# Pair results and two quarters of the token-major shares turned by DMA in a decoder trunk

## The chip, the cores and the metric

One core of one Trainium2 chip runs the whole kernel. The core has a TensorE (PE in the profile; PEld are its weight loads), a VectorE (DVE), a ScalarE (ACT), a GpSimd (POOL) and a SyncE (SP), which here only issues transfers; 16 DMA engines move data. The metric is the device time of the kernel in microseconds. Before the change it is 1678.69 us, the median of three runs (1678.51 to 1679.63).

## The reference

Two layers of a decoder trunk over 512 tokens of width 1024, in fp32:

```python
x = x + 0.5 * swiglu(rms_norm(x), wg1, wu1, wd1)       # feed-forward width 2816
z = rms_norm(x) @ w_in                                  # q, k, v and three conv parts
x = x + concat([attention(q, k, v), conv(...)]) @ w_out # sliding window 128, sinks, ALiBi
x = x + 0.5 * swiglu(rms_norm(x), wg2, wu2, wd2)
```

with `swiglu(h) = (silu(h @ wg) * (h @ wu)) @ wd` and a last RMSNorm after the two layers. So there are four feed-forwards. Nearly all the work is in their three weight matrices.

## The kernel before, in words

**Products.** Activations are held with features on the partitions ("feature-major", 128 features by 512 tokens a chunk); `xpair` holds the running x so, in four tiles of two chunks. Each fp32 factor is split in two: a rounded high part and the rest. A product is three matmuls (high x high, high x low, low x high). For the weights `split` (L212) does this: ScalarE casts the raw weight to `wh` (L213), VectorE subtracts to `wl` (L214). Three buffers each of `wh` and `wl` let the splits run two products ahead.

**Seven products for eight.** Most of a feed-forward is done by a scheme of Strassen's kind (as Winograd wrote it): 2 x 2 blocks of weights and activations are multiplied with seven block products, listed in `CHAINS` (L65). A stage therefore has seven *steps*, and each step two halves with 12 matmuls each per 128 columns of the other operand. `class Seven` (L554) makes the activation forms a step needs (`b11`, `b21`, `t1` to `t4`, `b22`), each split again by ScalarE and VectorE; `need_split` makes the weight forms, partly by transfers that add (issued by POOL, L208 and L279) and partly by VectorE (L249, L281).

**Stages of a feed-forward.** The lists `FIRST`, `INNER` and `LAST` (L32 to L40) name them. `p` and `d` are plain products up and down. A `w` stage (`winograd2`, L992), here called a *pair*, multiplies two blocks of the gate and up matrices; its results `ups[0..3]` come out *token-major* (128 tokens by 512 features each). An `s` stage (`share`, L822), a *shared stage*, multiplies two such pairs' results by the down matrix. The first feed-forward (`FIRST`) has four pairs, then one of another form (`u`) whose result needs no turning, and two shared stages. The two of `INNER` have five pairs and two shared stages; pairs 1, 3, 5 and 7 feed these, and pair 9 goes into the last plain down product. The last (`LAST`) has four such pairs as well, and its pair 9 goes into the closing stage `e`.

**Turning.** The down product needs its activations feature-major, so `turn` (L1047) turns each pair's result on TensorE: 16 transposes of 128 x 128 (L1050) into PSUM, then for pairs that feed shared stages a copy by ScalarE (L1057) into `raws[b]`, a tile of the pool `g8` (four buffers). For pair 9 of an inner feed-forward the PSUM tile is split straight into high and low (L1062). The 16 transposes are queued in `pending` and spread by `flush` over steps 0, 1 and 2 of the next pair (or over the next plain down product, or the next shared stage).

**Shares by tokens.** In the inner feed-forwards the shared stages' products come out token-major as well: `class Apart` (L856) sums them over both stages in eight tiles `y[t, o]`. Its `back(o, t)` (L870) turns one quarter (one half of the features, one half of the tokens) with eight transposes (L877) and adds it to x on VectorE (L883). `BACK_AT` puts three quarters into steps 2, 5 and 6 of the second shared stage, and the fourth follows in the last down product.

**What sets the order.** Each engine works through its own queue in order. A compile-time scheduler fills these queues: it takes the instructions in program order as priority, simulates when their inputs and buffers are ready, and moves an instruction ahead where its engine would be free. `tc.issue_after(i)` pins what is traced under it behind instruction `i` on that instruction's engine. SP issues all plain weight loads (L196) in its queue order, each as soon as one of the eight `raw` buffers is free. The pools that matter here are `g2` (14 tiles of 128 x 512 words), `g8` (4 tiles four times as large) and `xf` (14 tiles of 4 KB a partition).

Of the kernel before, what the change touches and what calls it, by code (L numbers as in the profile page):

```python
# [8 lines left out]
F32 = mybir.dt.float32  # L9
F32R = mybir.dt.float32r  # L10
BF16 = mybir.dt.bfloat16
I32 = mybir.dt.int32
AF = mybir.ActivationFunctionType
ALU = mybir.AluOpType

P = 128
D = 1024
S = 512
# [34 lines left out]

BACK_AT = {2: (0, 0), 5: (1, 1), 6: (1, 0)}
SCORES_AT = (5, 6, 7, 8, 9, 10, 12, 13)
# [16 lines left out]
def trunk_kernel(  # L72
# [55 lines left out]
    def f32(ap):  # L128
        return ap.bitcast(F32)


# [80 lines left out]
    def split(hi, lo, raw, eng=nc.vector):  # L212
        nc.scalar.copy(hi, raw)  # L213
        eng.tensor_sub(lo, raw, f32(hi))  # L214

    def split_far(hi, lo, raw):
# [5 lines left out]
    def need_split(g):  # L222
        while state["split"] <= min(g, len(order) - 1):
# [42 lines left out]
            if far:  # L266
                sent = split_far(hi, lo, raw)
            else:
                split(hi, lo, raw)
            if isinstance(order[n][1], tuple) and order[n][1][0] == "end":  # L270
# [283 lines left out]
    class Seven:  # L554
# [8 lines left out]
        def make(self, *names):  # L563
            for what in names:
                if what in self.forms:
                    continue
                b11, b12, b21, b22 = (
                    self.full[j][:, :, t * H : (t + 1) * H] for j in range(2) for t in range(2)
                )
# [286 lines left out]
    class Apart:  # L856


        def __init__(self, name):
            self.name, self.y = name, {}  # L860

        def add(self, t, o, acc, by):
# [5 lines left out]
            nc.vector.scalar_tensor_tensor(part, acc, by, part, op0=ALU.mult, op1=ALU.add)  # L868

        def back(self, o, t, tag="mm"):  # L870

            for m in range(2 * o, 2 * o + 2):
                tp = psum(tag, [P, 2, H], f"back_{self.name}_{m}_{t}")
                for j in range(2):
                    c = (2 * m + j) % NT
                    for u in range(2):
                        nc.tensor.transpose(  # L877
                            tp[:, j, u * P : (u + 1) * P],
                            self.y[2 * t + u, o][:, c * P : (c + 1) * P],
                            ident,  # L880
                        )
                part = xpair[m][:, :, t * H : (t + 1) * H]
                nc.vector.tensor_add(part, part, tp)  # L883
# [5 lines left out]
    def ffn(norm, stages, after=None, late=None):  # L889
# [102 lines left out]
        def winograd2(b, between=None):  # L992
# [49 lines left out]
            if b in blocks:  # L1042
                raws[b] = g8(f"raw_a_{name}", F32, (P, KC // 2, S))
            if b in few:
                raws[b] = [form(f"raw_a{n}_{name}", F32, (P, 2, S)) for n in range(2)]

            def turn(c, tag="sc"):  # L1047
                tp = psum(tag, [P, S], f"at_{name}_{c}")
                for t in range(NT):
                    nc.tensor.transpose(  # L1050
                        tp[:, t * P : (t + 1) * P], ups[t][:, c * P : (c + 1) * P], ident
                    )
# [3 lines left out]
                if b in raws:  # L1056
                    nc.scalar.copy(raws[b][:, c, :], tp)  # L1057
                    return
                if b + c // 2 not in acts:
                    acts[b + c // 2] = [form(f"a{n}_{name}_{c}", shape=(P, 2, S)) for n in "hl"]  # L1060
                hi, lo = acts[b + c // 2]
                split(hi[:, c % 2, :], lo[:, c % 2, :], tp)  # L1062

            pending.extend(lambda *tag, c=c: turn(c, *tag) for c in range(NT))

        def shared(b):
            return Seven([raws[b], raws[b + 2]], room_form, f"s_{norm.i}_{b}")

        def turns(step):

            if step < 2:
                flush()
            if step == 2:
                flush(2, "mm")

        sevens = [b for what, b in stages if what == "s"]
        blocks = [b + j for what, b in stages if what in "se" for j in (0, 2)]
        few = [b + 4 for what, b in stages if what == "e"]
        raws = {}
        pending = []  # L1080
# [8 lines left out]
        for i, (what, b) in enumerate(stages):  # L1089
# [10 lines left out]
            if what == "s" and end:  # L1100
                ends = [
                    Seven(full, None, f"e_{n}")
                    for n, full in enumerate(([raws[b + 4], raws[b + 6]], raws[b + 8]))
                ]
# [7 lines left out]

                share(ops, 0.5, between, apart)
            elif what == "e":
                end.last(ends)
                return
            elif what == "s" and b == sevens[0]:
# [3 lines left out]
                    0.5,  # L1121
                    ahead(then, {3: ("b11",), 4: ("b21",), 5: ("t2",), 6: ("t3",)}),
                    apart,
                )
            elif what == "s" and i + 1 == len(stages):
                share(then, 0.5, after.step)
            elif what == "s":

                def between(step):
                    if 2 <= step < 6:  # L1130
                        flush(1, "aux")
                    if step in BACK_AT:
                        apart.back(*BACK_AT[step])

                share(then, 0.5, between, apart)
# [10 lines left out]
            for c, acc in down(rhs, b == (0,) and not first, final):  # L1146
# [443 lines left out]
```

## Time and profile before

| | |
|---|---|
| median of three runs | 1678.69 us |
| the profiled execution's own time | 1678.83 us |
| its span | 1677.0 us |
| granted TensorE clock | 0.999 |
| busy: TensorE / VectorE / ScalarE / GpSimd | 99% / 83% / 58% / 13% of the span |
| DMA | 285.15 MB, mean 170 GB/s |

The span runs from the first to the last recorded instruction; the time of the execution is 1.8 us longer. A pair of an inner feed-forward takes about 40 us, a shared stage 38 to 42 us. In the rows of the profile a line such as L213 can be a helper's, so the names of the tiles (`wh`, `raw_a`, `at`, `back`, `apart`) say which use of it is meant. "x24" merges 24 instructions; in a chain of waits the second number is the time the chain spent there.

### The profile page before, as it was taken

How to read it: one execution, taken by the hardware profiler on the slowest of the kernel's cores; microseconds unless marked ns; L12 is line 12 of the kernel's file. 1: busy time of each engine (PE TensorE's matmuls, PEld its weight loads, DVE VectorE, ACT ScalarE, POOL GpSimd, SP SyncE). 2: the span in 40 equal slices, each digit the busy share in tenths (PEclk: the TensorE clock that was granted, in tenths of full speed). 3: DMA queues.
4: the chain of work that ended last, by engine and by line, in shares of the span. 5: the costliest groups of instructions: out<-in, count | busy, mean ns of one | idle time of the engine just before them, and what ended most of it. 6: DMA issues, size and time to landing. Idle time of an engine off the chain costs nothing.

```text
span 1677.0 us, 22346 instructions
## 1 busy us (share of the span) xinstructions
PE 1668.1 (99%) x8396; PEld 1414.0 (84%) x8396; DVE 1388.3 (83%) x1824; ACT 979.6 (58%) x1361; POOL 211.2 (13%) x188
## 2 busy tenths in 40 slices
PE   9999999999999999999999999999999999999998
PEld 7888889988898888888888888888888988888886
DVE  7987679988899976799798677997788998667997
ACT  6445565466566655575465555654565766556655
POOL 0011111001211111111011111110012111111121
PEclk9999999999999999999999999999999999999999
DMA  8467777731497777778567777785125967777892
GB/s 252 99 177 189 188 195 186 188 98 51 113 228 175 177 187 185 183 197 204 173 139 179 187 187 188 189 209 167 51 64 130 233 140 194 185 187 179 224 252 74
DMA packets 192545, 285.15 MB, mean 170 GB/s; under 512 B 9068, under 2 KB 77748, under 8 KB 192436
## 3 DMA queue, kind: packets, MB, share of 16 engines
q1 hardware_dynamic: 151844, 201.26, 38.1%
q0 software_dynamic: 39872, 81.80, 28.6%
q8 instruction: 66, 1.08, 0.3%
q10 hardware_dynamic: 720, 0.66, 0.1%
q14 instruction: 43, 0.35, 0.1%
HBM read 262.71 MB, written 2.10 MB: 158 GB/s over the span
## 4 chain that ended last, share of the span: by engine, by line
PE 96%; issue 1%; DMA 1%; DVE 1%; ACT 0%; POOL 0%; SPq 0%; POOLq 0%; DVEq 0%; ACTq 0%
PE x L813 25%; PE y L813 12%; PE acc L308 8%; PE acc L309 8%; PE acc L311 7%; PE x_s L813 6%; PE w L813 6%; PE y_s L813 3%; PE x_s L798 3%; PE at L1050 2%; PE x_m L798 2%; PE w_s L813 2%; PE y_s L798 1%; PE x_e L813 1%; PE y_m L798 1%; PE acc L693 1%
## 5 line engine op out<-in xcount | busy, mean ns | idle before, releaser
L213 ACT CAST wh<-raw 128x1024 fp32r<-128x1024 f32 (+1 forms) x491 | 513.0, 1045 | 535.8 <-PE x L813 129.1
L214 DVE TENSOR_TENSOR wl<-raw,wh 128x1024 fp32r<-128x1024 f32 (+1 forms) x491 | 598.3, 1221 | 202.8 <-ACT wh L213 201.2
L308 PE MATMUL acc<-xh,wh 128*128 128x512 f32 x424 | 165.8, 392 | 0.0
L309 PE MATMUL acc<-xl,wh 128*128 128x512 f32 x424 | 165.5, 390 | 0.0
L311 PE MATMUL acc<-xh,wl 128*128 128x512 f32 x416 | 162.3, 390 | 0.0
L208 POOL DMA_DIRECT2D raw<-in_ffn_wu_dram x39 | 48.9, 1254 | 419.7 <-DMA raw<-in_ffn_wu_dram 340.2
L309 PEld LDWEIGHTS acc<-xl,wh 128*128 128x128 f32 x424 | 79.7, 188 | 15.9 <-DVE xl L489 0.2
L308 PEld LDWEIGHTS acc<-xh,wh 128*128 128x128 f32 x424 | 79.8, 188 | 15.6
L311 PEld LDWEIGHTS acc<-xh,wl 128*128 128x128 f32 x416 | 78.1, 188 | 16.4
L208 POOL DMA_DIRECT2D raw<-in_ffn_wg_dram x39 | 48.0, 1255 | 221.1 <-DMA raw<-in_ffn_wu_dram 84.1
L208 POOL DMA_DIRECT2D raw<-in_ffn_wd_dram x34 | 41.0, 1207 | 259.4 <-DMA raw<-in_ffn_wd_dram 112.0
L249 DVE TENSOR_TENSOR raw<-raw,raw 128x1024 f32<-128x1024 f32 x56 | 68.0, 1219 | 2.4 <-DMA raw<-in_ffn_wu_dram 1.7
L813 PE MATMUL w<-wh,fb21h 128*128 128x512 f32 x152 | 60.7, 399 | 0.0
L813 PE MATMUL x<-wh,ft2h 128*128 128x512 f32 x152 | 60.6, 398 | 0.0
L813 PE MATMUL y<-wh,ft3h 128*128 128x512 f32 x152 | 60.4, 398 | 0.0
L813 PE MATMUL w<-wl,fb21h 128*128 128x512 f32 x152 | 59.4, 391 | 0.0
L813 PE MATMUL x<-wl,ft2h 128*128 128x512 f32 x152 | 59.3, 390 | 0.0
L813 PE MATMUL y<-wh,ft3l 128*128 128x512 f32 x152 | 59.2, 390 | 0.0
L813 PE MATMUL y<-wl,ft3h 128*128 128x512 f32 x152 | 59.2, 390 | 0.0
L813 PE MATMUL w<-wh,fb21l 128*128 128x512 f32 x152 | 59.2, 389 | 0.0
L813 PE MATMUL x<-wl,fb11h 128*128 128x512 f32 x152 | 59.2, 389 | 0.0
L813 PE MATMUL x<-wh,ft1l 128*128 128x512 f32 x152 | 59.1, 389 | 0.0
(602 smaller groups left out, 4586.4 us busy)
## 6 DMA issues: line engine op xcount, KB each, us to landing
raw<-in_ffn_wu_dram SPq DMA_DIRECT2D x126, 512.0 KB, 4.4
raw<-in_ffn_wd_dram SPq DMA_DIRECT2D x105, 512.0 KB, 5.7
raw<-in_ffn_wg_dram SPq DMA_DIRECT2D x86, 512.0 KB, 4.7
raw<-in_ffn_wu_dram POOLq DMA_DIRECT2D x39, 512.0 KB, 8.1
raw<-in_ffn_wg_dram POOLq DMA_DIRECT2D x39, 512.0 KB, 6.2
raw<-in_w_in_dram SPq DMA_DIRECT2D x36, 512.0 KB, 3.6
raw<-in_ffn_wd_dram POOLq DMA_DIRECT2D x34, 512.0 KB, 9.0
raw<-raw POOLq DMA_DIRECT2D x21, 512.0 KB, 8.3
```

Of the source, the lines that this page charges most:

```text
L208: nc.gpsimd.dma_start(out=r, in_=rows_of(*more), accum_op=ALU.add)
L213: nc.scalar.copy(hi, raw)
L214: eng.tensor_sub(lo, raw, f32(hi))
L249: nc.vector.tensor_add(a11, a11, s1)
L308: nc.tensor.matmul(acc, hi[:, k, :], rhs[k][0], start=k == first, stop=False)
L309: nc.tensor.matmul(acc, hi[:, k, :], rhs[k][1], start=False, stop=False)
L311: nc.tensor.matmul(acc, lo[:, k, :], rhs[k][0], start=False, stop=k == last)
L693: nc.tensor.matmul(opening[n], (lo if part == "w" else hi)[:, k, :], xl if part == "x" else xh, start=n not in begun, stop=k == KC - 1 and ...
L798: nc.tensor.matmul(accs[c // 2][:, c % 2, :], w[:, k, cols], x_[:, 2 * h + k, :], start=start and c % 2 == 0 and h + k + i == 0, stop=h + ...
L813: nc.tensor.matmul(accs[u], x_[:, 2 * h + k, tok], w[:, k, :], start=start and h + k + i == 0, stop=h + k == 2 and i == 2, skip_group_chec ...
L1050: nc.tensor.transpose(tp[:, t * P : (t + 1) * P], ups[t][:, c * P : (c + 1) * P], ident)
```

## The change

Turning is moved from TensorE to transfers. [...]

- `lay_apart` (new) copies a token-major tile on ScalarE into a `g2` tile of `(128, 2, 512)` 16-bit halves.
- `Crossing` (new) does this for the pairs that feed shared stages. In steps 0 and 1 of the next pair it lays two `ups` apart each and issues two DMA transposes on SP's queue into a `g8` tile; in steps 5 and 6 ScalarE joins the halves into `raws[b]`, pinned behind the last weight cast. For the last such pair of a feed-forward the join of all four chunks comes at step 3 of the first shared stage (`joined`).
- `Tail` (new) does it for pair 9 of the inner feed-forwards during the first shared stage: laid apart in steps 1 and 2, eight smaller transposes into two `xf` tiles, joined in steps 5 and 6. Its high and low parts are split in steps 2 and 4 of the second shared stage.
- `Apart.send` (new) does it for two quarters, (0, 0) at step 3 and (1, 1) at step 4 of the second shared stage. `back` joins them on ScalarE and adds them on VectorE: (1, 1) at step 6, and (0, 0) in the last down product. The other two quarters stay on TensorE.
- `Seven` takes its activations through a function, since `raws[b]` is there later than before.

Pair 9 of the last feed-forward keeps its TensorE transposes.

```diff
-BACK_AT = {2: (0, 0), 5: (1, 1), 6: (1, 0)}
+SENT_AT = {3: (0, 0), 4: (1, 1)}
...
+    def words(ap):
+        return ap.bitcast(U16).rearrange("p (n two) -> p two n", two=2)
+
+    def lay_apart(src, name):
+        halves = g2(f"halves_{name}", U16, (P, 2, S))
+        nc.scalar.copy(halves, words(src))
+        return halves
...
-        nc.scalar.copy(hi, raw)
+        cast = nc.scalar.copy(hi, raw)
         eng.tensor_sub(lo, raw, f32(hi))
+        return cast
...
+        def send(self, o, t):
+            to = self.sent[o, t] = g8(f"turned_{self.name}_{o}_{t}", U16, (P, 2, NT, H))
+            for u in range(2):
+                halves = lay_apart(self.y[2 * t + u, o], f"{self.name}_{o}_{2 * t + u}")
+                nc.sync.dma_start_transpose(
+                    to.rearrange("p a c s -> p (a c) s")[:, :, u * P : (u + 1) * P],
+                    halves.rearrange("p a n -> p (a n)"),
+                )
...
         def back(self, o, t, tag="mm"):
             for m in range(2 * o, 2 * o + 2):
+                part = xpair[m][:, :, t * H : (t + 1) * H]
+                if (o, t) in self.sent:
+                    whole = g2(f"back_{self.name}_{m}_{t}")
+                    j = 2 * (m - 2 * o)
+                    with tc.issue_after(state["cast"]):
+                        nc.scalar.copy(
+                            words(whole).rearrange("p two (c s) -> p two c s", c=2),
+                            self.sent[o, t][:, :, j : j + 2, :],
+                        )
+                    nc.vector.tensor_add(part, part, whole.rearrange("p (c s) -> p c s", c=2))
+                    continue
...
             if b in blocks:
-                raws[b] = g8(f"raw_a_{name}", F32, (P, KC // 2, S))
+                crossing.append(Crossing(b, name, ups))
+                return
+            if b in tails:
+                crossing.append(Tail(b, name, ups))
+                return
...
+        class Crossing:
+            def step(self):
+                n = self.steps
+                self.steps += 1
+                if n == 0:
+                    self.to = g8(f"turned_{self.name}", U16, (P, 2, NT, S))
+                for t in {0: (0, 1), 1: (2, 3)}.get(n, ()):
+                    halves = lay_apart(self.ups[t], f"{self.name}_{t}")
+                    nc.sync.dma_start_transpose(
+                        self.to.rearrange("p a c s -> p (a c) s")[:, :, t * P : (t + 1) * P],
+                        halves.rearrange("p a n -> p (a n)"),
+                    )
+                if n in (5, 6) and self.b != max(blocks):
+                    self.join(*((0, 1), (2, 3))[n - 5])
+                    return n == 6
+                return False
+
+            def join(self, *cs):
+                if self.b not in raws:
+                    raws[self.b] = g8(f"raw_a_{self.name}", F32, (P, KC // 2, S))
+                with tc.issue_after(state["cast"]):
+                    for c in cs:
+                        nc.scalar.copy(words(raws[self.b][:, c, :]), self.to[:, :, c, :])
+
+        class Tail:
+            def during(self, n):
+                if n == 1:
+                    self.to = [form(f"turned{h}_{self.name}", U16, (P, NT, S)) for h in range(2)]
+                for t in {1: (0, 1), 2: (2, 3)}.get(n, ()):
+                    halves = lay_apart(self.ups[t], f"{self.name}_{t}")
+                    for h in range(2):
+                        nc.sync.dma_start_transpose(
+                            self.to[h][:, :, t * P : (t + 1) * P], halves[:, h, :]
+                        )
+                if n == 5:
+                    self.whole = g8(f"raw_a_{self.name}", F32, (P, 2, 2, S))
+                if n > 4:
...
+            def parts(self, j):
+                hi, lo = acts[self.b + j] = [form(f"a{n}_{self.name}_{j}", shape=(P, 2, S)) for n in "hl"]
+                split(hi, lo, self.whole[:, j])
...
+        def joined(between):
+            def step(n):
+                if n == 3:
+                    crossing.pop(0).join(0, 1, 2, 3)
+                if crossing and isinstance(crossing[-1], Tail):
+                    crossing[-1].during(n)
+                between(n)
+            return step
...
                 def between(step):
-                    if 2 <= step < 6:
-                        flush(1, "aux")
-                    if step in BACK_AT:
-                        apart.back(*BACK_AT[step])
+                    if step in (2, 4):
+                        crossing[0].parts(step // 2 - 1)
+                    if step in SENT_AT:
+                        apart.send(*SENT_AT[step])
+                    if step == 6:
+                        apart.back(1, 1)
+                        apart.back(1, 0)
...
                 if final and c == KC // 2:
+                    apart.back(0, 0)
                     apart.back(0, 1, "sc")
```

More of the change, by code (lines that the diff above doesn't have):

```diff
@@ new lines, in ffn, with __init__, step @@
+        class Tail:
+            def __init__(self, b, name, ups):
+                self.b, self.name, self.ups = b, name, ups
+            def step(self):
+                return False
+            def during(self, n):
[10 more added lines that the diff above has]
+                if n > 4:
+                    whole = self.whole[:, n - 5].rearrange("p c s -> p (c s)")
+                    with tc.issue_after(state["cast"]):
+                        for h in range(2):
+                            nc.scalar.copy(
+                                words(whole)[:, h, :],
+                                self.to[h][:, 2 * (n - 5) : 2 * (n - 4), :].rearrange("p c s -> p (c s)"),
+                            )
+            def parts(self, j):
+                hi, lo = acts[self.b + j] = [form(f"a{n}_{self.name}_{j}", shape=(P, 2, S)) for n in "hl"]
+                split(hi, lo, self.whole[:, j])
@@ L1078, in ffn @@
         few = [b + 4 for what, b in stages if what == "e"]
+        tails = [b[0] for what, b in stages if what == "d" and len(b) == 2]
         raws = {}
@@ L1111, in between @@
                             ends[n].make(operand)
-                share(ops, 0.5, between, apart)
+                share(ops, 0.5, joined(between), apart)
             elif what == "e":
```

23 lines of the change are left out of this document (14 added, 9 removed).

## The prediction

> **What bounds the kernel now.** I read the page's first and fourth parts, then who waited for whom, then the chain piece by piece, then busy times by stage.
>
> ```profile
> span 1677.0 us, 22346 instructions
> PE 1668.1 (99%) x8396; PEld 1414.0 (84%) x8396; DVE 1388.3 (83%) x1824; ACT 979.6 (58%) x1361; POOL 211.2 (13%) x188
> PE 96%; issue 1%; DMA 1%; DVE 1%; ACT 0%; POOL 0%; SPq 0%; POOLq 0%; DVEq 0%; ACTq 0%
> PE x L813 25%; PE y L813 12%; PE acc L308 8%; PE acc L309 8%; PE acc L311 7%; PE x_s L813 6%; PE w L813 6%; PE y_s L813 3%; PE x_s L798 3%; PE at L1050 2%; PE x_m L798 2%; PE w_s L813 2%; PE y_s L798 1%; PE x_e L813 1%; PE y_m L798 1%; PE acc L693 1%
> PE idle L138 <- DVE warm L640: 1.2, 1, 1.2
> PE x_e L813 <- DVE bias L1206: 0.2, 1, 0.2
> ```
>
> TensorE is the chain (96%), and the view of waits knows only two waits of it, 1.4 us together. So every microsecond of TensorE work that goes is a microsecond of time, until another engine cannot keep the new pace. The transposes of L1050 are themselves a link of the chain, with 2%. Here is what they take out of a pair stage (chain by order of time), then out of the last shared stage, where those of L877 stand too:
>
> ```profile
> 585.51 0.44 PE at L1050 x4
> 585.95 5.50 PE w L813 x24
> 591.45 0.44 PE at L1050 x4
> 591.88 5.46 PE x L813 x24
> 597.35 0.87 PE at L1050 x8
> 598.22 5.46 PE y L813 x24
> 603.68 5.44 PE x L813 x24
> ...
> 794.18 0.44 PE at L1050 x4
> 794.62 0.87 PE back L877 x8
> ```
>
> A transpose holds the chain for 0.44/4 = 0.11 us (0.87/8 says the same). The product that follows one runs 5.50 or 5.46 us in place of 5.44. The views of the two lines give the counts and the length of one:
>
> ```profile
> L1050 PE MATMUL at<-ident,u x152: 270/271/273, 105.7 to 1589.8; 128*128 128x128 f32 x152
> L1050 PE MATMUL at<-ident,p x152: 272/272/327, 105.9 to 1590.0; 128*128 128x128 f32 x152
> L877 PE MATMUL back<-ident,apart x64: 270/272/273, 794.5 to 1158.1; 128*128 128x128 f32 x64
> ```
>
> 304 at L1050 are 16 for each of 19 pair stages; 64 at L877 are 8 for each of 8 quarters. A transpose lasts 0.27 us, but what counts is the 0.11 us, since the next instruction starts inside it.
>
> **The change, part by part.**
>
> *Off TensorE.* Eighteen of the 19 pair stages (16 that feed shared stages, two tails; the one before the kernel's end keeps its transposes) lose 16 each: 288 x 0.109 = 31.4 us. Two of four quarters in two feed-forwards lose 8 each: 32 x 0.109 = 3.5 us. The slower products after them: (0.06 + 0.02 + 0.02) = 0.10 us a stage, 18 x 0.10 = 1.8, and about 0.2 at the quarters. Together 36.9 us, all on the path.
>
> Busy time by stage (columns: stretch, length, then PE, PEld, DVE, ACT, POOL busy, clock, DMA share, GB/s) says what room the others have:
>
> ```profile
> 117.36:155.40 38.04, 38.04 (x170) 31.50 (x169) 27.49 (x30) 19.58 (x24) 4.14 (x4) 1.00 0.61 166
> 620.00:659.90 39.90, 39.90 (x185) 33.12 (x185) 27.76 (x30) 22.01 (x29) 3.62 (x5) 1.00 0.73 184
> 739.80:777.86 38.06, 38.06 (x169) 31.52 (x169) 37.04 (x37) 25.87 (x30) 6.34 (x6) 1.00 0.88 216
> 777.86:820.00 42.14, 42.14 (x206) 35.20 (x206) 33.77 (x40) 18.52 (x21) 4.20 (x4) 1.00 0.75 192
> 235.30:257.20 21.90, 21.90 (x187) 21.90 (x186) 20.86 (x25) 15.47 (x25) 3.24 (x4) 1.00 0.74 174
> 257.20:297.50 40.30, 40.30 (x337) 40.30 (x337) 39.80 (x43) 23.49 (x26) 4.96 (x5) 1.00 0.80 196
> ```
>
> In order: a pair stage without transposes (38.0 us), one with them (39.9; the difference is the 1.8 counted above), an inner feed-forward's first and second shared stage, and the first feed-forward's last pair with the shared stage behind it.
>
> *Onto ScalarE.* Each pair now costs four copies that lay the halves apart and four that join them, 1,024 elements of 16 bits a partition each, in place of four copies of 512 words.
>
> ```profile
> L213 ACT CAST wh<-raw 128x1024 fp32r<-128x1024 f32 x484 | 509.3, 1052 | 534.3 <-PE x L813 129.1 <-issue 93.4 <-PE y L813 84.2
> L1057 ACT COPY raw_a<-at 128x512 f32<-128x512 f32 x64 | 35.8, 586 | 3.1 <-PE at L1050 3.0
> L213 ACT CAST ah<-at x8: 579/580/583, 794.9 to 1147.9; 128x512 fp32r<-128x512 f32 x8
> 761.35 1.06 ACT L213 CAST wh<-raw 128x1024 fp32r<-128x1024 f32 x1 [0.54 <-PE y_s L813]
> 762.44 1.23 DVE L214 TENSOR_TENSOR wl<-raw,wh 128x1024 fp32r<-128x1024 f32 x1 [0.53 <-ACT wh L213]
> 766.98 5.44 PE y_s L813 x24
> ```
>
> By elements one copy costs 1.05 us, by bytes 0.59; I take 1.05 (the count of elements is the same) and keep 0.59 and 2.1 (twice, if the step of two halves costs) as ends. A pair stage then has 22.0 - 2.3 + 8 x 1.05 = 28.1 us of ScalarE in 38.1: hidden by the idle time ahead of the weight casts, 534 us over the kernel. The inner first shared stage has 25.9 + 12 x 1.05 (four joins of the fourth pair, four to lay apart and four to join the tail) = 38.5 in 38.1. That is full; what doesn't fit slides into the second shared stage, which has 18.5; there the tail's four 0.58 us casts become two of 1.05, and six copies for the quarters come on top: 18.5 - 2.3 + 2.1 + 6.3 = 24.6. The danger is the burst: four joins stand in a row (4.2 us) before the next weight cast. In this stage the cast at 761.35 and the subtraction behind it end at 763.67, 3.3 us before the product that reads them. A burst takes 4.2 us where about 1.7 were idle, so it costs 2.5 of the 3.3. I book 0.5 us at each of the four first shared stages, 2.0.
>
> *VectorE* gets nothing new but must keep the new pace. The first feed-forward's last pair shrinks to 20.1 us with 20.86 of VectorE in it, and the stage behind it has 39.8 in 40.3: 60.7 in 60.4 us. Most of that pair's 1.8 us stays lost: I book 1.5. In the ordinary pair stages it has 27.8 in 38.1, but bunched at the front; I book 0.1 us for each of 16, 1.6, and 0.5 for the last feed-forward's fifth pair. The joins put the shared stage's second operand (made two steps ahead of its place until now) back behind its step 3; its readers come in the next stage, so I cost that at nothing.
>
> *Onto the DMA engines.* A pair sends 4 x 256 KB, 1.05 MB; all of it 18 x 1.05 + 4 x 0.52 = 21 MB beside 285.
>
> ```profile
> q1 hardware_dynamic: 151844, 201.26, 38.1%
> q0 software_dynamic: 39872, 81.80, 28.6%
> raw<-in_ffn_wu_dram SPq DMA_DIRECT2D x126, 512.0 KB, 4.4
> raw<-in_ffn_wd_dram POOLq DMA_DIRECT2D x34, 512.0 KB, 9.0
> rows<-in_ffn_norm_dram ACTq DMA_DIRECT2D x1, 8.0 KB, 2.2
> ```
>
> No transposing transfer is in the trace. SP's plain loads moved 201.26 MB in 639 us of all engines, 315 GB/s; the adding ones 81.80 MB in 480 us, 171 GB/s. So 1.05 MB takes 3.3 to 6.1 us of all engines. I take 4, nearer the plain loads, since nothing is added. In a pair stage 0.73 x 39.9 = 29.1 + 4 = 33 of 38.1 us: hidden. In the inner first shared stage 33.5 + 4 = 37.5 of 38.1: hidden just so, with the lighter stages behind it as the overflow. Break-even is plain: a pair stage is as long as before when its transfers take 39.9 - 29.1 = 10.8 us, 97 GB/s.
>
> [...]
>
> *On SP's queue* come 4 transfers a pair, 8 a tail, 2 a quarter: 64 + 16 + 8 = 88.
>
> ```profile
> SPq L196 <- DVE wl L214: 1072.1, 298, 22.3
> L196 SPq DMA_DIRECT2D raw<-in_ffn_wu_dram x128: 367/368/2209, 4.3 to 1543.1; - x128
> L208 POOL DMA_DIRECT2D raw<-in_ffn_wu_dram x39: 1194/1203/1577, 32.0 to 1519.5; - x39
> ```
>
> At 0.37 us (SP's row) to 1.2 (POOL's) they hold SP 33 to 106 us, against 1072 us that it now waits for free weight buffers: hidden. But each waits for its copy on ScalarE, and the weight loads behind it in the queue wait with it; the adding loads (9.0 us to land), the products and ScalarE's casts come after those. The copies run two steps after their inputs are ready, so this wait is short: nothing booked. The joins wait for landings; between sending and joining lie four steps or more in a pair and a tail (22 us), and two in the tighter quarter (11 us), against 9.0.
>
> Sum: -36.9 + 2.0 + 1.5 + 1.6 + 0.5 = -31.3. Against the profiled execution's own 1678.8 us (span 1677.0 and 1.8 around it; the median of the runs, 1678.7, is the same within 0.1): 1647.5, say 1648 us.
>
> **The rivals.**
>
> *Partial gain: ScalarE or late weights eat half.* If the 16-bit copies cost 2.1 us each, a pair stage has 36.5 us of ScalarE in 38.1, and the inner first shared stage 51 in 38.1. Some 7 of the 13 us too much slide on, 6 stay, twice, and 8 to 10 more come from casts behind bursts in 16 pairs: about 20 us back, 1668. For it: the full shared stage. Against: ScalarE idles 534 us ahead of the casts.
>
> *Slower: the transfers are the bound.* Its place is every pair stage, its point 10.8 us for 1.05 MB. At four times the price of a plain load (pieces of 256 bytes might do that) it is 13.3 us, a stage of 29.1 + 13.3 = 42.4 in place of 39.9, 18 x 2.5 = 45 us slower, less the quarters' 3.5: 1720. SP's queue would show it first: a load behind such a transfer comes 3 us later each time. For it: even 8 KB took 2.2 us to land, and the DMA share is already 0.88 in one stage. Against: both rates in the trace lie well above 97 GB/s. Its far end would be squares that cross one after another, each like that 8 KB transfer: 32 x 2.2 = 70 us a pair, 18 x (29.1 + 70 - 39.9) = 1066 us slower, 2745; I give that 0.02 of this case's chance. [...]
>
> *No change:* transfers of 10.8 to 11.2 us a pair, where the stages merely trade one bound for another: 1676 to 1682.
>
> **How the numbers follow.** My forecast, 1642 (nothing lost) to 1656, has 0.63; the partial gain, 1656 to 1675, 0.14; no change 0.03; the slower case 0.20. A measurement here tells about 0.2% (3.4 us). So faster 0.77, same 0.03, slower 0.20. The range runs from 1640 to 1690: the first three cases hold 0.80 of the chance, and the part up to 1690 takes in the cheapest transfers beyond break-even, while the low end can hardly be passed, since 1642 is the whole of the work removed.
>
> **What would show it.** Right: pair stages of about 38.2 us, TensorE without waits, ScalarE near 67% of the span (979.6 + 130 over 1646), transposing transfers landing within 10 us, and the first feed-forward's last pair with VectorE at 95% or more. Wrong: waits of TensorE behind weight splits whose cast follows a join; ScalarE waiting for a turned tile; SP waiting for ScalarE in front of weight loads, with the adding loads late behind them; a DMA share at 1 through the pair stages.

## The result and the profile after

The changed kernel takes 1655.05 us, the median of four runs (1652.50 to 1655.83), beside 1678.61 us for the kernel before in the same session; the ratio is 0.9856, 95% interval 0.9839 to 0.9873. That is 23.6 us faster where 31.3 were forecast. The profile is of the slowest of the four runs, 1655.83 us.

The page of the changed kernel: span and busy times, the chain by engine, SP's queue, and the landing of the transposing transfers (issues, KB, us).

```profile
span 1654.1 us, 22072 instructions
PE 1636.2 (99%) x8076; PEld 1382.2 (84%) x8076; DVE 1381.4 (84%) x1820; ACT 1107.9 (67%) x1453; POOL 213.3 (13%) x188
...
PE 92%; DVE 4%; ACT 2%; issue 1%; DMA 1%; SPq 0%; DVEq 0%; ACTq 0%
...
q1 hardware_dynamic: 236580, 222.24, 46.7%
...
turned<-halves SPq DMA_TRANSPOSE x88, 5.1
```

TensorE lost 31.9 us of busy time (1668.1 to 1636.2). ScalarE gained 128 and stands at the forecast 67%. The transfers land in 5.1 us. But TensorE's share of the chain fell from 96% to 92%, and VectorE and ScalarE stand in it with 4% and 2%. An ordinary pair stage shows none of that (chain in order of time, the pair at 616 us):

```profile
621.61 5.44 PE w L825 x24
627.05 5.44 PE x L825 x24
632.49 5.44 PE y L825 x24
```

All transposes are gone and so are the slower products behind them; every step is 5.44 us. The busy times by stage of the changed kernel, for this pair and then for the first inner feed-forward's fifth pair, first and second shared stage (columns as in the prediction):

```profile
616.17:654.25 38.08, 38.08 (x169) 31.53 (x169) 27.70 (x30) 28.12 (x33) 4.04 (x4) 1.00 0.92 221
692.20:730.20 38.00, 38.00 (x169) 31.49 (x168) 35.36 (x37) 29.23 (x34) 4.82 (x4) 1.00 0.91 205
730.20:770.00 39.80, 38.75 (x170) 31.44 (x170) 29.85 (x30) 33.44 (x36) 6.65 (x6) 1.00 0.93 196
770.00:810.00 40.00, 38.29 (x166) 30.61 (x165) 37.44 (x39) 27.11 (x29) 4.17 (x4) 1.00 1.06 243
```

The pair is at 38.08 us with TensorE full, ScalarE at 28.1 as forecast. The first shared stage had 38.1 us and has 39.7 here (39.1 in the second inner feed-forward); TensorE idles 1.05 us in the first of these two windows and 1.7 in the next.

Where the time was lost is seen when the span is cut at the starts of the stages (each read off the trace as the first product with the form `fb11h`; us). "No loss" is the column of before less the TensorE work that the prediction took out of each stretch.

| stretch | before | no loss | after |
|---|---|---|---|
| A: first feed-forward, last pair and first shared stage | 73.1 | 71.3 | 76.6 |
| B: first inner one, fifth pair to the next feed-forward | 176.4 | 171.0 | 175.2 |
| C: second inner one, fifth pair to the next Strassen stage | 262.7 | 257.3 | 260.0 |
| D: last one, fifth pair to the end | 145.0 | 143.1 | 144.8 |
| all the rest | 1019.8 | 997.3 | 997.4 |

The rest gained nearly all it could, 22.4 of 22.5 us. In the four stretches around the first shared stages 13.9 us were lost: 5.3, 4.2, 2.7 and 1.7. Against the median of the four runs the loss is 36.9 - 23.6 = 13.3 us; a single execution can have 1 to 2 us more or less in a stretch.

Two views of the changed kernel show where. First the chain through the first shared stage of the first inner feed-forward:

```profile
748.72 1.88 ACT halves L138 x2
750.60 0.95 ACT wh L223
751.55 0.68 ACT raw_a L1133
...
753.75 3.65 ACT raw_a L1133 x3
757.40 0.91 ACT wh L223
...
758.33 1.24 DVE wl L224
...
759.61 5.05 PE y_s L825 x21
```

ScalarE is nearly all of the chain from 748 to 758: two copies that lay the tail apart, a weight cast, four joins (with sums of the token-major shares between them), and only then the next weight cast, VectorE's subtraction and the product. And in the first feed-forward's last pair, which is only 20 us long, VectorE's timeline (in brackets the idle time ahead and whom it waited for):

```profile
231.53 0.69 DVE L1069 TENSOR_TENSOR p<-p,gate 128x512 f32<-128x512 f32 x1 [0.97 <-ACT gate L1068]
232.47 1.23 DVE L224 TENSOR_TENSOR wl<-raw,wh 128x1024 fp32r<-128x1024 f32 x1 [0.25 <-ACT wh L223]
...
235.85 1.23 DVE L224 TENSOR_TENSOR wl<-raw,wh 128x1024 fp32r<-128x1024 f32 x1 [0.56 <-ACT wh L223]
...
240.25 1.23 DVE L224 TENSOR_TENSOR wl<-raw,wh 128x1024 fp32r<-128x1024 f32 x1 [1.70 <-ACT wh L223]
241.75 1.23 DVE L224 TENSOR_TENSOR fb21l_s<-raw_a,fb21h_s 128x1024 fp32r<-128x1024 f32 x1 [0.27 <-ACT fb21h_s L223]
```

VectorE waits 3.75 us for ScalarE, which is busy with the third pair's joins and the fourth pair's laying apart. From 243 on it is full, and TensorE comes to wait for it. Its windows (same columns as above), of that pair and then of the shared stage behind it, show what that costs:

```profile
229.80:250.00 20.20, 20.20 (x169) 20.15 (x168) 16.40 (x21) 17.51 (x25) 2.39 (x2) 1.00 0.91 193
...
257.00:264.80 7.80, 5.43 (x44) 5.03 (x42) 7.80 (x8) 4.09 (x4) 1.79 (x2) 1.00 0.76 138
264.80:272.20 7.40, 7.38 (x49) 7.38 (x50) 6.61 (x8) 2.03 (x3) 0.00 (x0) 0.77 0.94 230
...
265.34:268.76 3.42, 3.42 (x18) 3.42 (x18) 3.42 (x5) 0.00 (x0) 0.00 (x0) 0.50 1.12 208
```

VectorE is busy for 16.4 of the pair's 20.2 us. Then TensorE idles 2.4 of 7.8 us, and in the 7.4 us after that its granted clock is 0.77 on average, which costs another 1.7 (0.23 x 7.4). The last row shows what is in this average: 3.42 us at 0.50; the 3.44 us behind them are at 1.00 again. The idle time ahead of it comes in two pieces, 1.04 and 1.35 us.

The lower clock doesn't follow every time. These are the same stretches of the run below that leaves out the tail's transfers, an edit that does not touch the first feed-forward:

```profile
257.00:264.80 7.80, 5.42 (x43) 5.02 (x43) 7.80 (x9) 4.08 (x4) 1.79 (x2) 1.00 0.71 131
264.80:272.20 7.40, 7.40 (x64) 7.40 (x64) 7.40 (x9) 3.94 (x4) 0.00 (x0) 1.00 0.95 220
```

TensorE idles the same 2.4 us and keeps its clock, and stretch A takes 75.0 us in place of 76.6. The changed kernel's four runs have mean clocks of 0.997 to 0.999 over their spans, which fits a lower clock that comes in some of them only.

### The profile page after: what moved, and what is told of

It is laid out like the page before. It is cut to its first block, busy times and chain, and to the rows that moved or that the text cites. A ratio compares the mean times of both kernels' runs of the same rounds, so it can differ in the third digit from the quotient of the medians.

```text
span 1654.1 us, 22072 instructions
## 1 busy us (share of the span) xinstructions
PE 1636.2 (99%) x8076; PEld 1382.2 (84%) x8076; DVE 1381.4 (84%) x1820; ACT 1107.9 (67%) x1453; POOL 213.3 (13%) x188
## 3 DMA queue, kind: packets, MB, share of 16 engines
q1 hardware_dynamic: 236580, 222.24, 46.7%
## 4 chain that ended last, share of the span: by engine, by line
PE 92%; DVE 4%; ACT 2%; issue 1%; DMA 1%; SPq 0%; DVEq 0%; ACTq 0%
PE x L825 25%; PE y L825 12%; PE acc L319 8%; PE acc L320 8%; PE acc L322 8%; PE w L825 6%; PE x_s L825 5%; PE x_m L810 3%; PE y_s L825 3%; PE x_s L810 2%; DVE wl L224 1%; PE y_s L810 1%; PE y_m L810 1%; PE x_e L825 1%; PE acc L705 1%
## 5 line engine op out<-in xcount | busy, mean ns | idle before, releaser
L322 PEld LDWEIGHTS acc<-xh,wl 128*128 128x128 f32 x416 | 78.1, 188 | 16.4
L1133 ACT COPY raw_a<-turned 128x1024 uint16<-128x1024 uint16 x64 | 83.8, 1357 | 0.0
L825 PE MATMUL x<-wl,ft1h 128*128 128x512 f32 x152 | 59.2, 389 | 0.0
L825 PE MATMUL x<-wh,ft1h 128*128 128x512 f32 x152 | 59.1, 389 | 0.0
L825 PE MATMUL x<-wh,ft2l 128*128 128x512 f32 x152 | 59.1, 389 | 0.0
```

The source lines that it names most:

```text
L322: nc.tensor.matmul(acc, lo[:, k, :], rhs[k][0], start=False, stop=k == last)
L825: nc.tensor.matmul(accs[u], x_[:, 2 * h + k, tok], w[:, k, :], start=start and h + k + i == 0, stop=h + k == 2 and i == 2, skip_group_chec ...
L1133: nc.scalar.copy(words(raws[self.b][:, c, :]), self.to[:, :, c, :])
```

## The experiments

Two theories stood at the start. The first: the fourth pair's joins at step 3 of the first shared stage cost the time, by the burst on ScalarE or because the operand is late. The second: the transposing transfers do, by filling the DMA engines or SP's queue. The gains below are against the changed kernel's 1655.05 us; a pair's turn given back to TensorE costs 1.84 us (16 x 0.109, and 0.10 for the slower products). The kernel before took 1678.28 to 1678.61 us beside each of these runs. An edit also lets the compile-time scheduler order the queues anew, so that no run takes away one thing and leaves all else where it was.

### The fourth pair turned on TensorE again

```diff
-            if b in blocks:
+            if b in blocks and b != max(blocks):
                 crossing.append(Crossing(b, name, ups))
...
-                if n == 3:
-                    crossing.pop(0).join(0, 1, 2, 3)
```

> Only the last pair ahead of each first shared stage is turned on TensorE again, so the four joins in a row at step 3 of these stages are gone; all else as after the change. TensorE gets 4 x 1.8 = 7.2 us more. Theory A (the four joins in a row hold ScalarE's weight casts, and VectorE, full in that stage, loses what it waits): the 14 us lost around the four first shared stages mostly come back, 1655 + 7 - 10 to 14 = 1648 to 1652. Theory B (the transposing transfers overfill the DMA engines in the inner first shared stages and make the weights late): these stages keep their loss, the first and last feed-forward gain a little, 1658 to 1660.

Measured: 1650.33 us (1649.70 to 1650.86), ratio 0.9833 (0.9818 to 0.9848). It gives 4 x 1.84 = 7.4 us back to TensorE and is still 4.7 faster. With no loss at all it would take 1678.4 - 36.9 + 7.4 = 1648.9, so 1.4 us are left of the 14. Its stretches A to D take 73.2, 172.8, 259.9 and 144.9 us. Its windows for the fifth pair and the first shared stage of the first inner feed-forward, and then for the first feed-forward's last pair:

```profile
688.50:728.50 40.00, 40.00 (x186) 33.17 (x186) 36.54 (x37) 28.87 (x37) 5.63 (x5) 1.00 0.73 185
728.50:766.60 38.10, 38.10 (x170) 31.55 (x169) 33.88 (x35) 30.62 (x35) 5.78 (x6) 1.00 1.08 227
...
229.50:251.40 21.90, 21.90 (x186) 21.89 (x185) 20.13 (x24) 16.30 (x26) 3.87 (x4) 1.00 0.70 181
```

TensorE is full in all three. The DMA share is 1.08 in the first shared stage, higher than the changed kernel's 0.93, and TensorE does not wait. So the loss hangs on the fourth pair, and not on the tail's transfers, which are still there.

### The tail turned on TensorE again

```diff
-            if b in tails:
-                crossing.append(Tail(b, name, ups))
-                return
...
-                    if step in (2, 4):
-                        crossing[0].parts(step // 2 - 1)
+                    if 2 <= step < 6:
+                        flush(1, "aux")
```

> Only the tails (pair 9 of the two inner feed-forwards) are turned on TensorE again: eight transposing transfers and eight copies less in each inner first shared stage, the burst of four joins stays. TensorE gets 2 x 1.8 = 3.6 us more. Theory A: the burst still stands, about half of the inner stages' 7 us comes back, 1655 us. Theory B: the DMA engines have room again in the inner shared stages, their 7 us come back whole, 1651 to 1652.

Measured: 1654.40 us (1653.47 to 1655.46), ratio 0.9860 (0.9843 to 0.9876): no different. Two turns given back cost 3.7 us, so some 4 of the loss went. The tail's laying apart and joining stand in the first shared stage beside the fourth pair's joins, so without them ScalarE has less to do there; the next experiment but one shows that the transfers were not what helped.

### Joins that write in order

```diff
-                        nc.scalar.copy(words(raws[self.b][:, c, :]), self.to[:, :, c, :])
+                        nc.scalar.copy(
+                            raws[self.b][:, c, :].bitcast(U16).rearrange("p (n two) -> p n two", two=2),
+                            self.to[:, :, c, :].rearrange("p a s -> p s a"),
+                        )
```

> The joins of the pairs write their words in order and take the step in what they read, in place of writing every other half word; same number of copies and of elements. If the written step is what makes a join 1.36 us and not 1.05, a join falls to about 1.05 and the burst from 5.1 to 4.0 us. Theory A: a little over 1 us back in each first shared stage, 1650 to 1652. Theory B: no change, 1654 to 1656. If the copy stays at 1.36 us, it says nothing between them.

The copies of the changed kernel (min/median/max in ns), and then the join's group in this one (busy us, mean ns):

```profile
L138 ACT COPY halves<-u x36: 1034/1046/1085, 122.4 to 1517.0; 128x1024 uint16<-128x1024 uint16 x36
L1133 ACT COPY raw_a<-turned x64: 1336/1357/1377, 146.4 to 1572.7; 128x1024 uint16<-128x1024 uint16 x64
```

```profile
L1133 ACT COPY raw_a<-turned 128x1024 uint16<-128x1024 uint16 x64 | 72.8, 1174 | 0.0
```

Measured: 1651.24 us (1650.17 to 1652.59), ratio 0.9839 (0.9824 to 0.9854), 3.8 us faster. The same copy takes 1.17 us in place of 1.36 when it writes in order and reads with a step. 64 x 0.18 us are 12 us of ScalarE, of which the ordinary pairs, without loss before, can have given nothing back. In the profiled execution A to D take 75.4, 173.4, 259.5 and 144.2 us, 4.2 less together than in the changed kernel's, and the rest 0.9 more: there the gain lies around the bursts, each 0.7 us shorter. In A the third pair's joins, which reach into the last pair, are shorter too; that was not tried apart.

### The tail without its transfers

```diff
-                    for h in range(2):
-                        nc.sync.dma_start_transpose(
-                            self.to[h][:, :, t * P : (t + 1) * P], halves[:, h, :]
-                        )
```

> The tails' transposing transfers are left out and their joins read a constant, so pair 9 of the inner feed-forwards does not reach the output; ScalarE's and VectorE's instructions stay the same in number and size, only 2 x 8 transfers go. Theory A: as after the change, 1654 to 1656. Theory B: the inner stages' 7 us come back, 1647 to 1649.

The tail's joins then read zeros in place of the turned halves. Measured: 1654.05 us, a single run, within the changed kernel's runs. So no cost of the tail's transfers and of their places on SP's queue is seen.

### The quarters turned on TensorE again

```diff
-SENT_AT = {3: (0, 0), 4: (1, 1)}
+SENT_AT = {}
...
+                    if step == 2:
+                        apart.back(0, 0)
+                    if step == 5:
+                        apart.back(1, 1)
                     if step == 6:
-                        apart.back(1, 1)
...
-                    apart.back(0, 0)
```

> The two quarters are turned on TensorE again, the pairs and tails stay with the transfers: TensorE gets 32 x 0.109 = 3.5 us more, ScalarE 16 copies less in the inner second shared stages. Both theories: 1657 to 1659 if the quarters' copies cost nothing there; 1653 to 1655 if ScalarE and VectorE, behind after the first shared stage, are held by them.

Measured: 1658.54 us (1656.92 to 1660.04), ratio 0.9881 (0.9866 to 0.9896), 3.5 us slower. The quarters' part of the change brings about what was forecast for it, 3.5 and 0.2 for the slower products.

### The joins in two portions

```diff
                 if n == 3:
-                    crossing.pop(0).join(0, 1, 2, 3)
+                    crossing[0].join(0, 1)
+                if n == 4:
+                    crossing.pop(0).join(2, 3)
```

> The fourth pair's four joins are parted: two at step 3 and two at step 4 of the first shared stage, each two behind a later weight cast. Number, size and price of the copies stay; the joined tile is ready later than after the change. Theory A1 (the burst itself: ScalarE is held 5 us at a stretch while weight casts are due): most of the 14 us come back, 1644 to 1648. Theory A2 (the lateness: the second shared stage's operands can only be made after the join, and their work piles up on a full VectorE): nothing comes back or more is lost, 1655 to 1660.

Measured: 1659.75 us (1659.18 to 1663.51), ratio 0.9893 (0.9878 to 0.9908), 4.7 us slower. The first shared stage is back at 38.1 us, and the second loses more. The chain there:

```profile
756.85 1.61 SPq L1152
...
758.57 5.09 DMA raw<-in_ffn_wd_dram
...
764.25 10.41 DMA raw<-in_ffn_wd_dram
...
777.11 1.15 DVE wl L224
...
778.30 7.58 PE w_s L825 x20
```

Now a weight load queued on SP behind the tail's transfers is late, and the adding load behind it takes 10.4 us. The product then runs 20 instructions in 7.58 us in place of 24 in 5.44, at half the clock:

```profile
777.40:784.20 6.80, 5.90 (x14) 4.65 (x15) 6.59 (x7) 1.04 (x1) 1.76 (x2) 0.50 1.11 208
```

A burst in two portions moves the loss to another place.

### Four copies beside the fourth pair on TensorE

The first experiment, with four copies of a join's form at step 3 whose results nothing reads:

```diff
+                if n == 3:
+                    spare = g8(f"spare_{norm.i}", F32, (P, KC // 2, S))
+                    with tc.issue_after(state["cast"]):
+                        for c in range(NT):
+                            nc.scalar.copy(words(spare[:, c, :]), ...)
```

> As the run with the fourth pair on TensorE (1650.3 us), but with four copies of the joins' size on ScalarE at step 3 of the first shared stages that nothing reads: the burst without the lateness, 16 copies or 22 us of ScalarE work over the kernel. A1: the loss comes back, 1659 to 1664. A2: it stays at 1650 to 1652.

Measured: 1656.75 us (1656.31 to 1658.23), ratio 0.9873 (0.9857 to 0.9890): 6.4 us over the first experiment, on average 1.6 for each first shared stage; in the profiled execution A to D are 0.7, 2.8, 2.0 and 1.5 us longer than there. The chain has the figure of the changed kernel, with `spare` for `raw_a`:

```profile
746.59 1.88 ACT halves L138 x2
...
751.61 1.64 ACT spare L1187 x2
...
753.91 1.36 ACT spare L1187
755.27 0.91 ACT wh L223
...
756.20 1.24 DVE wl L224
```

So the burst costs time by itself, without any operand that is late and without the fourth pair's transfers. This is its price beside a longer pair; in the changed kernel it may be another.

### The joins on GpSimd

```diff
-                    crossing.pop(0).join(0, 1, 2, 3)
+                    ...
+                    for c in range(NT):
+                        nc.gpsimd.tensor_copy(words(raws[late.b][:, c, :]), late.to[:, :, c, :])
```

> The fourth pair's four joins are made by GpSimd, which is idle most of the time, in place of ScalarE. No trace here has such a copy; its row for two operands of 128x512 words is 1.3 to 1.5 us, so 1.3 to 3 us each. A1: ScalarE has no burst, the 14 us come back, 1642 to 1647, if the copies do not hold the adding loads behind them in GpSimd's queue. A2: the join is as late or later, 1655 to 1660.

```profile
L1182 POOL COPY raw_a<-turned 128x1024 uint16<-128x1024 uint16 x16 | 28.1, 2108 | 0.0
```

Measured: 1662.19 us (1658.03 to 1663.34), ratio 0.9898 (0.9884 to 0.9913), 7.1 us slower. A join takes 2.11 us there, four 8.4, in the queue that also issues the adding loads; the inner first shared stages take 41 us.

### A part of the operand late, without a burst

The first experiment, with the last of the fourth pair's four groups of transposes, and its copy, held back to step 3:

```diff
             if step == 2:
+                if ... len(pending) == 2 and not held:
+                    held.append(pending.pop())
                 flush(2, "mm")
...
+                if n == 3:
+                    held.pop()("mm")
```

> The fourth pair is turned on TensorE, as in the run that did this before (1650.3 us), but the last of its four groups of transposes, with its one copy on ScalarE (0.59 us in the kernel before), is held back to step 3 of the first shared stage: the second operand is as late as with the joins, and the burst is gone. Theory that the burst of 5.4 us on ScalarE is the whole cause: 1650 to 1652, the stage behind the first shared stage as in that run. Theory that the operand's lateness costs as much as the burst does: 1655 to 1658, with the loss in the second shared stages.

Measured: 1650.42 us (1650.19 to 1650.67), ratio 0.9832 (0.9818 to 0.9847), the same as the first experiment. That a quarter of the operand comes as late as step 3, and with it every form made of it, costs nothing.

### The joins left out

```diff
                 if n == 3:
-                    crossing.pop(0).join(0, 1, 2, 3)
+                    late = crossing.pop(0)
+                    raws[late.b] = raws[late.b - 2]
```

> The changed kernel without the four joins at step 3 of the first shared stage: the fourth pair is still laid apart and sent, but never read, and its shared stages take the third pair's words a second time in its place (so the output lacks the fourth pair). TensorE, the transfers, SP's queue and VectorE have the changed kernel's work. Theory that the joins (their burst and their lateness) are the whole loss: 1642 to 1645, the sum of the work removed. Theory that laying apart and sending the fourth pair, or the faster pace alone, have a part in it: 1646 to 1651. Transfers as the cause: 1653 or more.

Measured: 1656.74 us (1654.45 to 1658.95), ratio 0.9870 (0.9855 to 0.9884). Both theories about the joins fall as a full account: without them the kernel is no faster. The stretches A to D of the profiled execution take 75.9, 176.8, 264.1 and 143.1 us. D has no loss any more; there taking the joins away gives all of it back. In A and B the loss stays, and C loses more. Windows of this kernel, for the first feed-forward's last pair and the 16 us behind it, then for a wait in the first inner one's second shared stage and the time after:

```profile
229.60:249.80 20.20, 20.20 (x169) 20.13 (x168) 16.39 (x21) 17.50 (x25) 2.39 (x2) 1.00 0.88 176
249.80:265.80 16.00, 13.63 (x110) 13.23 (x110) 16.00 (x18) 8.79 (x11) 4.20 (x4) 0.99 0.76 176
...
771.00:777.60 6.60, 2.59 (x12) 1.82 (x10) 3.56 (x4) 2.56 (x3) 2.41 (x2) 0.99 0.84 192
777.60:784.40 6.80, 6.72 (x23) 5.48 (x24) 6.80 (x8) 2.05 (x3) 1.76 (x2) 0.76 1.11 211
```

In the first feed-forward VectorE does 16.4 us of work in the last pair; with the fourth pair on TensorE it did 20.1 in 21.9 us. It goes into the shared stage 3.7 us behind, is full there, and TensorE idles 2.4 us. In the inner one VectorE does 35.4 of the 36.5 us that it did in the longer pair, and the wait comes later and is longer: 4.0 us, and 0.24 x 6.8 = 1.6 more by the clock. The chain there goes over an adding load; why this wait is longer without the joins than with them is open:

```profile
759.24 5.27 DMA raw<-in_ffn_wd_dram
...
765.11 10.07 DMA raw<-in_ffn_wd_dram
...
777.68 6.76 PE w_s L825 x22
```

### Joins in order, and only the first feed-forward's fourth pair on TensorE

The edit of the third experiment (for the quarters too), and the first experiment's where `first` holds.

> The changed kernel with joins that write the words in order and read with a step (pairs and quarters), and with the first feed-forward's fourth pair turned on TensorE. If the two gains of the runs before add up (3.8 us for the order, 2.2 us for the first feed-forward's stretch up to its second shared stage): 1649. If the order's gain lay mostly in the first feed-forward, 1651 to 1652.

Measured: 1648.84 us (1648.39 to 1649.02), ratio 0.9823 (0.9806 to 0.9839). The two gains add up, and this is the fastest of all, 6.2 us ahead of the changed kernel. A to D: 73.1, 173.3, 259.5 and 144.0 us. A is 3.5 us shorter than in the changed kernel, the 1.84 us of TensorE given back included.

### The joins without the fourth pair's transfers

```diff
                     halves = lay_apart(self.ups[t], f"{self.name}_{t}")
+                    if self.b == max(blocks):
+                        continue
```

> The changed kernel without the four transposing transfers of the fourth pair: it is still laid apart in the next pair and still joined by four copies at step 3, but the copies read zeros (so the output lacks the fourth pair). ScalarE, VectorE and TensorE have the changed kernel's work; only these 16 transfers and their places in SP's queue are gone. The run without the joins, 1656.7 us, sent them; there, and in the changed kernel, the adding loads of the pair before the first shared stage land in 11.6 to 12.8 us against 8.5 where the fourth pair is not sent. Theory that these transfers make the adding loads late, and that this is a cause beside the burst: the adding loads land in about 8.5 us and start as in the kernel before, and only the burst is left, 1643 + 6.4 = 1649, within 1647 to 1652. Theory that the shorter pair (38.1 us with 35.4 of VectorE) is that cause, with the transfers hidden: 1654 to 1658, as with them.

The fourth pair's joins then read zeros. Measured: 1656.82 us (1654.06 to 1657.94), ratio 0.9873 (0.9857 to 0.9890). So the fourth pair's transfers are no cause of the loss. Of the adding loads in the fifth pair of the first inner feed-forward, the changed kernel has the first of these rows and this one the second:

```profile
raw<-in_ffn_wd_dram POOLq DMA_DIRECT2D x2, 512.0 KB, 12.8
```

```profile
raw<-in_ffn_wd_dram POOLq DMA_DIRECT2D x2, 512.0 KB, 9.6
```

They land 3.2 us earlier, and the time is no shorter. A to D take 76.3, 173.8, 260.1 and 144.8 us, as in the changed kernel but for 1.4 in B; B is 173.8 in the run without the tail's transfers too, so that the changed kernel's profiled execution is the one that stands out there.

## Why the prediction was right, and where it was not

**Off TensorE, 36.9 us: right.** The rest of the kernel gained its part (22.4 of 22.5 us), the quarters about theirs, and without loss the sum would have come out.

**The size of the loss: this step failed.** "I book 0.5 us at each of the four first shared stages, 2.0", with 1.5 for the first feed-forward's last pair and 0.5 for the last one's: 4.0 us in the four stretches, where 13.9 were lost. Three things are in it.

- *The burst was too cheap.* Four joins are 4 x 1.36 = 5.4 us by their lengths and 4.9 by the chain's pace (3.65 us for three), and not 4.2, and the slack of one product (3.3 us) was taken as free for it, though the tail's laying apart stands there too. Four such copies beside the fourth pair on TensorE cost 1.6 us a stage on average, 6.4 in all.
- *The pair ahead was read off the wrong row.* The prediction took VectorE's room in a pair from an ordinary one, 27.8 us. The pair ahead of a shared stage also makes that stage's forms: in the changed kernel it has 35.4 in 38.0 us, against 27.7 in the ordinary pair. The kernel before has 36.5 in 39.9 us there (row below). For the inner feed-forwards' fifth pairs no more than 0.1 us each was booked on its account. For the first feed-forward the fullness was seen, and booked at 1.5; that stretch lost 5.3, and it lost 4.6 without the joins too. There VectorE does not run at "95% or more", as forecast: it has 16.4 us in 20.2, because ScalarE's copies hold up the casts that it waits for, and the work left over falls into the next stage.
- *A wait cost more than its length.* In the changed kernel's profiled execution 2.4 us of idle TensorE were followed by 1.7 us lost to the lower clock; without the joins 4.0 were followed by 1.6. In the run without the tail's transfers the same 2.4 us cost nothing more. The prediction had no such term.

The first inner feed-forward's fifth pair in the kernel before (columns as in the prediction):

```profile
699.70:739.60 39.90, 39.90 (x185) 33.14 (x184) 36.51 (x37) 27.61 (x35) 3.66 (x4) 1.00 0.73 185
```

**What was booked and not lost:** 0.1 us for each of 16 pair stages. They are at 38.08 us, and VectorE's bunching costs nothing there.

**The transfers: hidden, as forecast, though dearer.** SP's queue moved 20.98 MB more in 133.5 us more of all engines (46.7% of 1654.1 less 38.1% of 1677.0): 157 GB/s, or 6.7 us a pair, if the plain loads on it took as long as before. That is outside the ends of 3.3 and 6.1 and within the break-even of 10.8, and twice the price of a plain load (315 GB/s in the kernel before). The rival of the transfers put four times, which no run shows, and named pieces of 256 bytes; the 84,736 packets more on that queue have 248 bytes on average. Its far end, 70 us for a pair's 32 squares one after another, is far off. Leaving out the tail's or the fourth pair's transfers changed nothing.

**The late operand: nothing, as forecast**, by the run with one part late, as far as that run goes: it holds back a quarter of the operand.

**SP's queue: nothing booked, and nothing seen in the changed kernel's loss.** When the joins were parted, the chain did go over it.

**The rival of a partial gain** named the right places (casts behind bursts, the full first shared stage) and the wrong price: 2.1 us a copy and 1668 us. One of the signs that the prediction would take as wrong, a wait behind a weight split whose cast follows a join, is in the chain at 757 us. The result lies in the forecast's own range, 1642 to 1656, at its upper end. That end was not worked out from any row, and with 13 us lost in place of 5.6 it is in part luck that the result fell inside it.

**What stays open.** The loss is gone only where the fourth pair is turned on TensorE, which does three things: no joins, no laying apart in the pair ahead, and that pair 1.84 us longer. The joins are one cause (6.4 us by themselves; D is free of loss without them), but not the only one, for without them A to C keep the loss. Whether there the laying apart or the shorter pair weighs more was not tried apart. VectorE's rows in A speak for both: of the 3.7 us that it is behind, 1.7 are the shorter pair (20.2 for 21.9) and 2.0 are more idle time in it (3.8 for 1.8).

## What to carry to other kernels

When an engine at 99% is relieved, look for the stage in which the next engine has least room, and take its busy time from that stage's own row: here 35.4 of 38.0 us where ordinary stages had 27.7. Work that moves to an engine with much idle time should not come as a burst in front of what feeds that stage; average room (busy for 67% of the span) says nothing about it. And a helper that frees the bound engine can be left out at the few places where it does harm: one pair turned the old way and a cheaper order of the same copy brought 6.2 us more than the full change.

## What the runs showed of the hardware

- A copy of 1,024 16-bit elements a partition took ScalarE 1.04 us where it reads with a step of two and writes in order within each plane, 1.17 where it interleaves two planes and writes in order, and 1.36 where it writes every second half-word. On GpSimd the last took 2.11 us. Three of the 1.36 us kind behind one another held ScalarE's chain for 3.65 us.
- DMA transposes from SBUF to SBUF moved an estimated 157 GB/s beside other traffic, from what SP's queue gained (20.98 MB in 133.5 us of all engines). One of a pair held SP's queue 1.24 us (median of 64); a plain load held it 0.37.
- TensorE idle for 2.4 of 7.8 us was followed by 3.42 us at a granted clock of 0.50 in the changed kernel's profiled execution, and by none in that of the run without the tail's transfers. When the joins were parted, 6.8 us at 0.50 followed a wait.
